# An MLP up projection by seven block products, with the weight sums made by adding DMAs

## The chip, the cores and the metric

The kernel runs on one core of one Trainium2 chip. The metric is the device time of one execution in microseconds, the median of several runs. A profile of one execution has a row for each instruction of the engines: TensorE (PE, its weight loads PEld), VectorE (DVE), ScalarE (ACT), GpSimd (POOL) and SyncE (SP, which issues DMAs).

## What is computed

One layer of a hybrid backbone over 512 latent tokens and 256 context tokens, model width 2048, in float32. The layer projects the modulated tokens, runs bidirectional GLA and mLSTM scans, gates and projects the result back, and adds it to the residual stream. Then follows the MLP, which the change is about:

```python
def conv_ffn(h, rows, cols, w_up, conv_w, conv_b, w_down):
    u = jnp.einsum('btd,df->btf', h, w_up)            # 512 x 2048 by 2048 x 11008
    u_gate, u_val = jnp.split(u, 2, axis=-1)          # 5504 columns each
    g = lax.conv_general_dilated(u_gate.reshape(b, rows, cols, D_FF), ...)   # 3x3 depthwise, 8 x 64 grid
    g = g.reshape(b, t, D_FF) + conv_b
    return jnp.einsum('btf,fd->btd', jax.nn.silu(g) * u_val, w_down)
...
    h2 = rmsnorm(x, g_norm2) * (1 + sc2) + sh2
    x = x + gt2 * conv_ffn(h2, rows, GRID_W, w_up, conv_w, conv_b, w_down)
```

The shifts, scales and gates (sh, sc, gt) come from a vector times a 2048 x 12288 matrix, six regions of 2048 columns. A final RMSNorm ends the kernel.

## The kernel before

All activations lie transposed: 128 channels on the partitions, 512 tokens along a row, so the 2048 channels are 16 tiles (k). A float32 product is made by three faster ones (`mm3`): each operand is split into a high part (`hi`, a cast on ScalarE, line 89) and a low part (`lo`, the rest, a subtraction on VectorE, line 90), and high by high, high by low and low by high are summed in PSUM. `load_split` fetches 512 KB of weights (two k, 512 columns) on SP's queue into one of four buffers `wraw` (tag "raw") and splits it into one of two buffers `whi` and `wlo`. So a split can start only when the chunk two before has been used up, and it has the time of one chunk to be ready.

`unit` runs eight such chunks over four PSUM tiles of 512 tokens: 8 x 4 x 2 x 3 = 192 matmuls. The MLP has 43 column tiles of 128 gate and 128 value columns, taken four at a time: a unit `ug` for the gate, a unit `uv` for the value. Between them VectorE and ScalarE convolve (`cv`: a first tap on ScalarE, eight on VectorE at line 1043, one after another on the same tile), and the product with the value is split into `gh` and `gl`. After two such rounds `down_block` (`dn`) multiplies the eight finished tiles with the down weights, in four blocks of 512 outputs, and `residual` adds them to the stream `x2`, which stays in SBUF. The tail `dl` does the last block in two parts of the tokens so that the norm can begin early.

Beside this run the "fillers": the modulation regions 2 to 5 are sums over weight rows (`raw_m`, `sum_m`), made by VectorE, ScalarE and POOL from 512 KB loads, with a `rate` that says how many fillers a weight chunk brings along. Regions 2, 3 and 4 run beside the heads and the gate and output projections (`ga`, `wo`), region 5 beside the first units of the MLP. Their loads use the same `wraw` buffers as the weights.

A scheduler orders the instructions of each engine at build time, by program order and priority; a waiting instruction then holds up those behind it on its engine.

Of the kernel before, what the change touches and what calls it, by code (L numbers as in the profile page):

```python
# [11 lines left out]
F32 = mybir.dt.float32  # L12
F32R = mybir.dt.float32r
# [5 lines left out]
P = 128  # L19
# [17 lines left out]
QUADS = [4] * 10 + [3]  # L37
GROUPS = [[0, 1], [2, 3], [4, 5], [6, 7], [8, 9, 10]]
# [31 lines left out]
def block_kernel(ctx: ExitStack, tc: tile.TileContext, a: dict, out: bass.AP):  # L70
# [48 lines left out]
    actp = pool(ctx, "actp")  # L119
    yp = pool(ctx, "yp")  # L120
    psA = pool(ctx, "psA", 6, PSUM)
# [16 lines left out]
    def ytile(k, name, shape=(P, T)):  # L138
        return yp.tile(list(shape), F32, name=name, tag=f"y{k}")
# [18 lines left out]
    rate, credit = [0], [0]  # L158

# [82 lines left out]
    def mod_chunk(region, n, kp, parts):  # L242

        name = f"m{region}_{n}_{kp}"
        raw = wraw.tile([P, 2, T], F32, name=f"raw_{name}", tag="raw")
# [12 lines left out]
        if kp == KP - 1:  # L258
            G.tensor_tensor(out=po, in0=po, in1=dv, op=ALU.add)
# [616 lines left out]
    mod_fillers((2, 3, 4), 3)  # L876
# [34 lines left out]
    for h in range(1, 2 * H):  # L911
        if h + 1 < 2 * H:
            accs = [acc(f"a{h + 1}_{g}", BANKS[g]) for g in range(6)]
            steps = project_steps(h + 1, accs)
        else:
            rate[0] = 1.5
# [15 lines left out]
    rate[0] = 1.5  # L932
# [19 lines left out]
    def residual(k, ps, gate, sl=slice(0, T)):  # L952
        xx = x2[k][:, sl]
        V.scalar_tensor_tensor(out=xx, in0=ps, scalar=gate[:, k : k + 1], in1=xx, op0=ALU.mult, op1=ALU.add)
# [27 lines left out]

    sums2 = []
    for n in range(4):
        accs = unit(a["w_out"][n], f"wo{n}", yh, yl)
        with tc.high_priority():
            for i in range(4):
                residual(4 * n + i, accs[i], modc[2])
                square(4 * n + i, sums2, rp, "sq")
# [3 lines left out]
    h2 = ([], [])  # L993
    with tc.high_priority():
        for k in range(KT):
            t = gp.tile([P, T], F32, name=f"h2_{k}", tag="h2")
            sk, bk = modc[4][:, k : k + 1], modc[3][:, k : k + 1]
            h2[0].append(acttile(k, "h", f"h2h{k}"))
            h2[1].append(acttile(k, "l", f"h2l{k}"))
            mul(t, x2[k], r2)  # L1000
            S.activation(h2[0][k], t, AF.Identity, scale=sk, bias=bk)  # L1001
            V.tensor_scalar(out=t, in0=t, scalar1=sk, scalar2=bk, op0=ALU.mult, op1=ALU.add)
            sub(h2[1][k], t, h2[0][k].bitcast(F32))
    st_3.close()
    st_h.close()


    fp = pool(ctx, "fp")
    tp = pool(ctx, "tp", 4)
# [4 lines left out]
    pads = [fp.tile([P, ROWS + 2, GW + 2], F32, name=f"pad{i}") for i in range(4)]  # L1014
    for p in pads:
        G.memset(p, 0.0)
    gs = {}
    LAST = 4 * GROUPS[-1][0]
    glast = fp.tile([P, NF - LAST, P], F32, name="glast")

    def sum_tile(i, name):
        return fp.tile([P, T], F32, name=f"sum{i}_{name}", tag=f"g{'hl'[i]}10")

    rate[0] = 1.5
    fillers += [lambda: None] * 20
    mod_fillers((5,), 2)

    def up_gate(q):
        accs = unit(a["w_up4"][2 * q] if q < 10 else a["w_up3"][0], f"ug{q}", *h2, n=QUADS[q])
        convs = []  # L1030
        for i, ps in enumerate(accs):
            f = 4 * q + i
            with tc.high_priority():
                S.copy(pads[i][:, 1 : ROWS + 1, 1 : GW + 1], ps.rearrange("p (r c) -> p r c", c=GW))
            t = tp.tile([P, T], F32, name=f"cv{f}", tag="cv")
            t3 = t.rearrange("p (r c) -> p r c", c=GW)
            for tap in range(9):
                src = pads[i][:, tap // 3 : tap // 3 + ROWS, tap % 3 : tap % 3 + GW]
                w = cwt[:, f, tap : tap + 1]
                if tap == 0:  # L1040
                    S.activation(t3, src, AF.Identity, scale=w, bias=cbt[:, f : f + 1])  # L1041
                else:
                    V.scalar_tensor_tensor(out=t3, in0=src, scalar=w, in1=t3, op0=ALU.mult, op1=ALU.add)  # L1043
            S.activation(t, t, AF.Silu)
            convs.append(t)
        return convs

    def up_val(q, convs):
        accs = unit(a["w_up4"][2 * q + 1] if q < 10 else a["w_up3"][1], f"uv{q}", *h2, n=QUADS[q])
        for i, ps in enumerate(accs):  # L1050
            f = 4 * q + i
            with tc.high_priority():
                mul(convs[i], convs[i], ps)
                gh = fp.tile([P, T], F32R, name=f"gh{f}", tag=f"gh{f % 8 if q < 10 else 8 + i}")
                gl = fp.tile([P, T], F32R, name=f"gl{f}", tag=f"gl{f % 8 if q < 10 else 8 + i}")
                split(gh, gl, convs[i])
            gs[f] = (gh, gl)
            if f >= LAST:
                S.copy(glast[:, f - LAST, :], convs[i][:, 3 * P :])

    def fspan(qs):
        return [f for q in qs for f in range(4 * q, 4 * q + QUADS[q])]

    def down_block(fs, blk):
        accs = [acc(f"dn{fs[0]}_{blk}_{i}") for i in range(4)]
        for p in range(0, len(fs), 2):
            pair = fs[p : p + 2]
            wh, wl = load_split(a["w_down"][blk][:, pair[0] : pair[0] + len(pair), :], f"d{pair[0]}_{blk}", n=len(pair))
            for i in range(4):
                for ff, f in enumerate(pair):  # L1070
                    mm3(accs[i], wh[:, ff, P * i : P * i + P], wl[:, ff, P * i : P * i + P],
                        gs[f][0], gs[f][1], f == fs[0], f == fs[-1])
        with tc.high_priority():
            for i in range(4):
                residual(4 * blk + i, accs[i], modc[5])

    todo = list(GROUPS)
    for q in range(len(QUADS)):
        convs = up_gate(q)
        if len(todo) > 1 and q > todo[0][-1]:  # L1080
            assert not fillers
            for blk in range(4):
                down_block(fspan(todo[0]), blk)
            todo.pop(0)
        up_val(q, convs)
# [3 lines left out]
    fs = fspan(todo[0])  # L1089
    parts = [slice(0, 3 * P), slice(3 * P, T)]  # L1090
    sums3 = [[], []]
    for blk in range(3):
        down_block(fs, blk)
        for k in range(4 * blk, 4 * blk + 4):
            for pt, sl in enumerate(parts):
                square(k, sums3[pt], fp, f"fq{pt}", sl)
            S.activation(x2[k], x2[k], AF.Copy, scale=gnf[:, k : k + 1])

    wd = []
    for n, f in enumerate(fs):  # L1100
        if n < 10:
            raw = actp.tile([P, T], F32, name=f"raw_dl{f}", tag=f"a{'hl'[n % 2]}{11 + n // 2}")
        else:
            raw = fp.tile([P, T], F32, name=f"raw_dl{f}", tag="wlast")
        wh, wl = acttile(n, "h", f"dlh{f}"), acttile(n, "l", f"dll{f}")
# [5 lines left out]
    for pt, sl in enumerate(parts):  # L1111
# [10 lines left out]
        with tc.high_priority():  # L1122
            for i in range(4):
                residual(12 + i, accs[i], modc[5], sl)
                square(12 + i, sums3[pt], fp, f"fq{pt}", sl)
            r3 = token_rstd(sums3[pt], fp, f"rmsf{pt}", w)
            r3s = fp.tile([P, w], F32, name=f"r3s{pt}", tag=f"r3s{pt}")
# [17 lines left out]
def arrange(x, c, ctx, c_ctx, w_mod, b_mod, g_norm1, g_norm2, w_in, gla_w_lr, gla_b_lr, mlstm_b_gate,  # L1145
# [44 lines left out]
    for d in range(2):  # L1190
# [3 lines left out]
    r["w_up4"] = np.stack([blocks(w_up[:, FF * s + 512 * q : FF * s + 512 * q + 512], 512)  # L1194
                           for q in range(10) for s in range(2)])
    r["w_up3"] = np.stack([blocks(w_up[:, FF * s + 5120 : FF * s + 5504], 384) for s in range(2)])
# [20 lines left out]
```

## Time and profile before

| | |
|---|---|
| median of 3 runs | 2596.1 us (2593.98 to 2598.04) |
| profiled execution | 2598.67 us, its span 2597.0 us |
| PE busy | 2530.0 us, 97%, 12782 matmuls |
| DVE, ACT, POOL busy | 1361.3, 873.7, 225.8 us |
| granted TensorE clock, mean | 0.993 |
| DMA | 321.96 MB, mean 124 GB/s |
| MLP | from 1163.5 us to the end |

Busy times of matmuls overlap: a row's duration is longer than the pace at which such rows follow each other. So the pace is read from the starts of neighbouring rows, or from a stretch with its count. A row of the groups has line, engine, operation, output and inputs, shape and count, then busy time and mean duration in ns, then the idle time before it and what ended it. Names of tiles have their buffer numbers left out.

### The profile page before, as it was taken

What the parts mean: (1) busy time and instruction counts of PE and PEld (TensorE: products, weight loads), DVE (VectorE), ACT (ScalarE), POOL (GpSimd) and SP (SyncE); (2) the same over time, 40 slices, a digit from 0 to 9 for tenths busy, and PEclk for the clock granted to TensorE, in tenths of its full rate; (3) what the DMA queues carried; (4) which work ended last, traced back from release to release, by engine and by line L of the source; (5) the groups of instructions that cost most, each with busy time, mean ns of one, the idle gap of its engine ahead of it and who ended that gap; (6) DMA issues with size and microseconds to landing.
All of it is one profiled execution on the core that took longest, in us unless ns stands there. A gap on an engine that the chain in (4) does not pass through costs nothing.

```text
span 2597.0 us, 31782 instructions
## 1 busy us (share of the span) xinstructions
PE 2530.0 (97%) x12782; PEld 2132.0 (82%) x12782; DVE 1361.3 (52%) x1972; ACT 873.7 (34%) x1289; POOL 225.8 (9%) x179
## 2 busy tenths in 40 slices
PE   6998999999999999999999999999999999999998
PEld 4887898888897887878878888888888888888887
DVE  6566765543344465458576326533653365336643
ACT  4224543333334344334443123312331233123431
POOL 0000000111212323210321000000000000000000
PEclk9999999999999999989999999999999999999999
DMA  8751012231333566633554333333233323333431
GB/s 322 282 204 41 30 44 81 69 96 64 130 119 126 205 233 221 192 121 100 208 186 138 97 98 98 98 97 97 98 97 96 96 95 97 97 97 90 141 90 65
DMA packets 96676, 321.96 MB, mean 124 GB/s; under 512 B 11152, under 2 KB 15504, under 8 KB 96528
## 3 DMA queue, kind: packets, MB, share of 16 engines
q1 hardware_dynamic: 95376, 319.40, 37.5%
q8 instruction: 100, 1.64, 0.3%
q10 hardware_dynamic: 1152, 0.52, 0.1%
q14 instruction: 48, 0.39, 0.0%
HBM read 315.69 MB, written 4.19 MB: 123 GB/s over the span
## 4 chain that ended last, share of the span: by engine, by line
PE 89%; DVE 5%; DMA 3%; issue 1%; ACT 1%; SPq 0%; POOL 0%; DVEq 0%; ACTq 0%; POOLq 0%
PE ug L95 18%; PE uv L95 17%; PE dn L95 17%; PE a L95 16%; PE wo L95 6%; PE ga L95 5%; PE po L95 3%; DMA raw_m<-in_w_mod 2%; PE sl L95 1%; PE dl L95 1%; PE ps_m L95 1%; DVE cv L1043 1%; DMA raw_h<-in_w_heads 1%; PE s L95 0%; PE cst L95 0%
## 5 line engine op out<-in xcount | busy, mean ns | idle before, releaser
L95 PE MATMUL ug<-h2h,hi_ug 128*128 128x512 f32 x688 | 269.0, 392 | 1.6 <-ACT h2h L1001 1.6
L95 PE MATMUL uv<-h2h,lo_uv 128*128 128x512 f32 x688 | 268.8, 391 | 1.6 <-DVE lo_uv L90 1.6
L95 PE MATMUL uv<-h2h,hi_uv 128*128 128x512 f32 x688 | 268.6, 390 | 1.2 <-ACT hi_uv L89 1.2
L95 PE MATMUL ug<-h2l,hi_ug 128*128 128x512 f32 x688 | 268.3, 390 | 0.0
L95 PE MATMUL uv<-h2l,hi_uv 128*128 128x512 f32 x688 | 268.2, 390 | 0.0
L95 PE MATMUL ug<-h2h,lo_ug 128*128 128x512 f32 x688 | 268.2, 390 | 0.0
L95 PE MATMUL dn<-gh,hi_d 128*128 128x512 f32 x644 | 250.5, 389 | 0.0
L95 PE MATMUL dn<-gl,hi_d 128*128 128x512 f32 x644 | 250.5, 389 | 0.0
L95 PE MATMUL dn<-gh,lo_d 128*128 128x512 f32 x644 | 250.5, 389 | 0.0
L1043 DVE SCALAR_TENSOR_TENSOR cv<-pad,cwt,cv 128x512 f32<-128x512 f32 x344 | 242.5, 762 | 10.6 <-ACT cv L1041 9.1
L90 DVE TENSOR_TENSOR lo_ug<-raw_ug,hi_ug 128x1024 fp32r<-128x1024 f32 (+1 forms) x88 | 106.5, 1210 | 240.1 <-ACT hi_ug L89 240.1
L257 POOL TENSOR_TENSOR sum_m<-sum_m,raw_m 128x512 f32<-128x512 f32 x112 | 175.3, 1566 | 578.2 <-ACT raw_m L256 358.4
L90 DVE TENSOR_TENSOR lo_uv<-raw_uv,hi_uv 128x1024 fp32r<-128x1024 f32 (+1 forms) x88 | 105.9, 1203 | 177.5 <-ACT hi_uv L89 177.1
L90 DVE TENSOR_TENSOR lo_d<-raw_d,hi_d 128x1024 fp32r<-128x1024 f32 x82 | 98.8, 1205 | 166.5 <-ACT hi_d L89 165.5
L89 ACT CAST hi_ug<-raw_ug 128x1024 fp32r<-128x1024 f32 (+1 forms) x88 | 90.9, 1033 | 266.6 <-PE ug L95 196.4
L89 ACT CAST hi_d<-raw_d 128x1024 fp32r<-128x1024 f32 x82 | 85.0, 1037 | 280.4 <-PE dn L95 231.8
L255 DVE SCALAR_TENSOR_TENSOR sum_m<-raw_m,csil,sum_m 128x512 f32<-128x512 f32 x112 | 97.6, 871 | 156.1 <-DMA raw_m<-in_w_mod 155.9
L89 ACT CAST hi_uv<-raw_uv 128x1024 fp32r<-128x1024 f32 (+1 forms) x88 | 90.9, 1033 | 246.4 <-PE uv L95 181.3
L95 PEld LDWEIGHTS uv<-h2h,lo_uv 128*128 128x128 f32 x688 | 129.4, 188 | 30.2 <-DVE lo_uv L90 3.2
L95 PEld LDWEIGHTS ug<-h2h,hi_ug 128*128 128x128 f32 x688 | 129.8, 189 | 28.8 <-ACT h2h L1001 1.9
L95 PEld LDWEIGHTS uv<-h2h,hi_uv 128*128 128x128 f32 x688 | 129.5, 188 | 28.3 <-ACT hi_uv L89 1.6
L95 PEld LDWEIGHTS ug<-h2h,lo_ug 128*128 128x128 f32 x688 | 129.6, 188 | 27.2
(308 smaller groups left out, 5178.7 us busy)
## 6 DMA issues: line engine op xcount, KB each, us to landing
raw_m<-in_w_mod SPq DMA_DIRECT2D x192, 512.0 KB, 4.4
raw_ug<-in_w_up SPq DMA_DIRECT2D x80, 512.0 KB, 3.4
raw_uv<-in_w_up SPq DMA_DIRECT2D x80, 512.0 KB, 3.4
raw_d<-in_w_down SPq DMA_DIRECT2D x79, 512.0 KB, 3.5
raw_h<-in_w_heads SPq DMA_DIRECT2D x64, 512.0 KB, 3.4
raw_ga<-in_w_gates SPq DMA_DIRECT2D x32, 512.0 KB, 4.3
raw_wo<-in_w_out SPq DMA_DIRECT2D x32, 512.0 KB, 4.3
xl<-in_xT SPq DMA_DIRECT2D x16, 256.0 KB, 5.1
```

Source lines behind the costliest of these rows:

```text
L89: S.copy(hi, x)
L90: return V.tensor_tensor(out=lo, in0=x, in1=hi.bitcast(F32), op=ALU.subtract).ins
L95: ins = PE.matmul(*args, **kw)
L255: V.scalar_tensor_tensor(out=dv, in0=raw[:, 0, :], scalar=ce, in1=dv, op0=ALU.mult, op1=ALU.add)
L257: G.tensor_tensor(out=po, in0=po, in1=raw[:, 1, :], op=ALU.add)
L1043: V.scalar_tensor_tensor(out=t3, in0=src, scalar=w, in1=t3, op0=ALU.mult, op1=ALU.add)
```

## The change

Each of the last 39 column tiles f is now a 2 x 2 block product: the 2048 input channels in two halves, gate and value as the other two halves of the weights, and the 512 tokens in two halves of 256. Seven products of 1024 channels by 128 columns by 256 tokens (numbered 0 to 6 in the code) and some sums replace eight. Four sums are of weights, four of tokens (made once, `token_sums`, into `bt`), and the rest are of results. The first four column tiles are done plainly (`up_two`), while the token sums are made.

The weight sums are made by DMAs that add to their target, issued by POOL: s1 (its second load added from DRAM), s3 (likewise), then a11 += s1 and a12 += a11 from tiles in SBUF to tiles in SBUF. Product 6 of a tile is put behind product 0 of the next one (`pending`), so TensorE's order is 0 of f, 6 of f - 1, then 1, 3, 2, 5, 4 of f. Before a down block it is not put off. A down group now has seven column tiles (the last one eight).

To make room, the residual stream is written to DRAM (`x2d`) after the output projection; each down block loads four tiles of it into `stage`, adds, and stores them. The last group loads all sixteen back (`x3`). Region 5 of the modulation moves into the gate and output projections, which get four raw buffers of their own for these loads (`mraw3`) and a rate of 2 and 2.25 in place of 1.5.

```diff
-    mod_fillers((2, 3, 4), 3)
+    mod_fillers((2, 3, 4, 5), 3)
...
+    modraw[0] = pool(st_3, "mraw3", 4)
+    rate[0] = 2.25
...
+                residual(x2[k], k, accs[i], modc[2])
+                square(k, sums2, rp, "sq")
+                nc.sync.dma_start(x2d[k], x2[k])
...
+    def up_seven(f, pending):
+        def load(q, i, j, **kw):
+            eng = G if kw else nc.sync
+            eng.dma_start(q, a["w_up"][f - FIRST, i, j].rearrange("p k c -> p (k c)"), **kw)
+        a11, a12, a22 = (wraw.tile([P, KH * P], F32, name=f"q{f}_{n}", tag="raw") for n in range(3))
+        s1, s3 = spare[0][:, f % 2, :], spare[1][:, 0, :]
+        load(s1, 1, 0)
+        load(a11, 0, 0)
+        load(s1, 1, 1, accum_op=ALU.add)
+        load(s3, 1, 0)
+        load(a12, 0, 1)
+        load(s3, 0, 0, accum_op=ALU.add)
+        load(a22, 1, 1)
+        def product(n, src, o, first):
+            wh = whi.tile([P, KH * P], F32R, name=f"hi_q{f}_{n}", tag="hi")
+            wl = wlo.tile([P, KH * P], F32R, name=f"lo_q{f}_{n}", tag="lo")
+            with tc.high_priority():
+                split(wh, wl, src)
+            for k in range(KH):
+                c = slice(P * k, P * k + P)
+                mm3(o, wh[:, c], wl[:, c], *operands[n](k), first and k == 0, k == KH - 1, skip_group_check=True)
...
+        product(0, a11, x, True)
+            S.copy(p1, x)
+        pending()
+        product(1, a12, w, True)
+        G.dma_start(a11, s1, accum_op=ALU.add)
+        G.dma_start(a12, a11, accum_op=ALU.add)
+            add(pad[:, 1 : ROWS // 2 + 1, 1 : GW + 1], rows(w), rows(p1))
+        product(3, s1, v, True)
+            S.copy(p5, v)
+        product(2, a11, x, False)
+            S.copy(u2, x)
+        product(5, a12, v, False)
+            add(pad[:, ROWS // 2 + 1 : ROWS + 1, 1 : GW + 1], rows(v), rows(u2))
+        product(4, s3, x, False)
+            neg_add(val[:, hi], x, p5)
+        def last():
+            product(6, a22, x, False)
+                S.activation(val[:, lo], x, AF.Copy, scale=-1.0)
+            conv(f, pad, val)
+        return last
...
+    def down_block(fs, blk):
+        for i in range(4):
+            nc.sync.dma_start(stage[i], x2d[4 * blk + i])
+        accs = down_products(fs, blk)
+                residual(stage[i], 4 * blk + i, accs[i], modc[5])
+                nc.sync.dma_start(x2d[4 * blk + i], stage[i])
```

VectorE in the middle of the MLP, before, at the end of a value unit (`uv5`) and the start of the next gate unit (`ug6`): `lo_` are the splits, `cv` the convolutions of column tiles 20 to 23, `gl` the low parts of their results.

```order
L1043 SCALAR_TENSOR_TENSOR cv23_13713<-pad3_9430,cwt_9423,cv23_13713 128x512
L90 TENSOR_TENSOR lo_uv5_6_13910<-raw_uv5_6_13908,hi_uv5_6_13909 128x1024
L90 TENSOR_TENSOR lo_uv5_7_13940<-raw_uv5_7_13938,hi_uv5_7_13939 128x1024
L90 TENSOR_TENSOR lo_ug6_0_13994<-raw_ug6_0_13992,hi_ug6_0_13993 128x1024
L83 TENSOR_TENSOR cv20_13677<-cv20_13677,uv5_0_13724 128x512
L83 TENSOR_TENSOR cv21_13689<-cv21_13689,uv5_1_13725 128x512
L90 TENSOR_TENSOR gl20_13970<-cv20_13677,gh20_13969 128x512
```

VectorE now, in one column tile (13): `lo_q13_n` is the split for product n, `cv12` the convolution of the tile before (two, three, two and one taps in a row), `val12` and `pad1` the sums out of PSUM.

```order
L90 TENSOR_TENSOR lo_q13_0_13087<-q13_0_13072,hi_q13_0_13086 128x1024
L1081 SCALAR_TENSOR_TENSOR cv12_13144<-pad0_9546,cwt_9542,cv12_13144 128x512 x2
L1042 SCALAR_TENSOR_TENSOR val12_12850<-x12_12847,part_p5_9648 128x256
L90 TENSOR_TENSOR lo_q12_6_13116<-q12_2_12839,hi_q12_6_13115 128x1024
L1081 SCALAR_TENSOR_TENSOR cv12_13144<-pad0_9546,cwt_9542,cv12_13144 128x512 x3
L90 TENSOR_TENSOR lo_q13_1_13161<-q13_1_13073,hi_q13_1_13160 128x1024
L1081 SCALAR_TENSOR_TENSOR cv12_13144<-pad0_9546,cwt_9542,cv12_13144 128x512 x2
L90 TENSOR_TENSOR lo_q13_3_13192<-spareh_10502,hi_q13_3_13191 128x1024
L1081 SCALAR_TENSOR_TENSOR cv12_13144<-pad0_9546,cwt_9542,cv12_13144 128x512
L86 TENSOR_TENSOR pad1_9547<-w13_13083,part_p1_9647 128x4x64
L90 TENSOR_TENSOR lo_q13_2_13221<-q13_0_13072,hi_q13_2_13220 128x1024
L83 TENSOR_TENSOR cv12_13144<-cv12_13144,val12_12850 128x512
```

The splits stand in the order of the products, and the taps are dealt out between them.

POOL before, from the end of the fillers to the final norm: in between it has nothing.

```order
L257 TENSOR_TENSOR sum1_m5_3_0_10735<-sum1_m5_3_0_10735,raw_m5_3_7_10918 128x512
L259 TENSOR_TENSOR sum1_m5_3_0_10735<-sum1_m5_3_0_10735,sum0_m5_3_0_10734 128x512
L1138 TENSOR_TENSOR x2_2_7960<-x2_2_7960,r3s0_18539 128x384
L1138 TENSOR_TENSOR x2_5_7978<-x2_5_7978,r3s0_18539 128x384
L1138 TENSOR_TENSOR x2_8_7996<-x2_8_7996,r3s0_18539 128x384
```

POOL now, in the column tiles 12 and 13: `spareh` is s1, `sparel` is s3, `q13_0` is a11 and `q13_1` is a12 of tile 13.

```order
L1121 DMA spareh_10502<-in_w_up 128x1024
L1153 DMA q12_0_12837<-spareh_10502 128x1024
L1121 DMA sparel_10503<-in_w_up 128x1024
L1154 DMA q12_1_12838<-q12_0_12837 128x1024
L1121 DMA spareh_10502<-in_w_up 128x1024
L1153 DMA q13_0_13072<-spareh_10502 128x1024
L1121 DMA sparel_10503<-in_w_up 128x1024
L1154 DMA q13_1_13073<-q13_0_13072 128x1024
```

Each tile has four adding DMAs on this queue; the one into s3 stands between the two on tiles in SBUF, and the s1 of the next tile behind them.

More of the change, by code (lines that the diff above doesn't have):

```diff
@@ L981, in token_rstd @@
         return o
+    dr = pool(ctx, "dr", 1, bass.MemoryType.DRAM)
+    x2d = [dr.tile([P, T], F32, name=f"x2d{k}", tag=f"x2d{k}") for k in range(KT)]
     sums2 = []
@@ L992, in block_kernel @@
     assert not fillers
[L993 to L1003, printed above, removed]
     st_3.close()
     st_h.close()
+    st_a.close()
+    KH, TH = KT // 2, T // 2
     fp = pool(ctx, "fp")
-    tp = pool(ctx, "tp", 4)
+    tp = pool(ctx, "tp", 2)
     cwt = fp.tile([P, NF, 9], F32, name="cwt")
@@ L1013, in block_kernel @@
     nc.sync.dma_start(cbt, a["conv_b"])
-    pads = [fp.tile([P, ROWS + 2, GW + 2], F32, name=f"pad{i}") for i in range(4)]
+    pads = [fp.tile([P, ROWS + 2, GW + 2], F32, name=f"pad{i}") for i in range(2)]
     for p in pads:
         G.memset(p, 0.0)
-    gs = {}
[L1018 to L1032, printed above, removed]
-            with tc.high_priority():
[L1034 to L1051, printed above, removed]
-            with tc.high_priority():
[L1053 to L1059, printed above, removed]
@@ new lines, in block_kernel @@
+    with tc.high_priority():
+        for k in range(KT):
+            t = x2[k]
+            sk, bk = modc[4][:, k : k + 1], modc[3][:, k : k + 1]
+            mul(t, t, r2)
+            for sl, (h, l) in halves(k):
+                S.activation(h, t[:, sl], AF.Identity, scale=sk, bias=bk)
+            V.tensor_scalar(out=t, in0=t, scalar1=sk, scalar2=bk, op0=ALU.mult, op1=ALU.add)
+            for sl, (h, l) in halves(k):
+                sub(l, t[:, sl], h.bitcast(F32))
+    assert not fillers
@@ L1100, in block_kernel @@
     for n, f in enumerate(fs):
[L1101 to L1105, printed above, removed]
+        raw = gp.tile([P, T], F32, name=f"raw_dl{f}")
+        wh, wl = (gp.tile([P, T], F32R, name=f"dl{i}{f}") for i in "hl")
         nc.sync.dma_start(raw, a["w_down"][3][:, f, :])
```

159 lines of the change are left out of this document (127 added, 32 removed).

## The prediction

> **What bounds the kernel now.** I read the page first for the engine that carries the span, then the chain that ended last in order of time, then the stretch in which the MLP runs.
>
> ```profile
> span 2597.0 us, 31782 instructions
> PE 2530.0 (97%) x12782; PEld 2132.0 (82%) x12782; DVE 1361.3 (52%) x1972; ACT 873.7 (34%) x1289; POOL 225.8 (9%) x179
> PE 89%; DVE 5%; DMA 3%; issue 1%; ACT 1%; SPq 0%; POOL 0%; DVEq 0%; ACTq 0%; POOLq 0%
> ```
>
> TensorE is 89% of the chain. In the MLP it is nearly all of it; these rows of the chain have start, length, engine and tile:
>
> ```profile
> 1163.54 46.03 PE ug L95 x192
> ...
> 1289.00 5.18 DMA raw_m<-in_w_mod
> ...
> 1393.25 87.04 PE dn L95 x384
> 1480.29 43.52 PE uv L95 x192
> 1523.81 43.52 PE ug L95 x192
> ```
>
> From 1393 on, units of four accumulators follow each other without a gap. 192 matmuls of 512 columns take 43.52 us, so the pace is 43.52/192 = 0.2267 us. (A row's own duration, 0.39 us, is longer because matmuls overlap.) Before 1393 the five units from 1163.54 to 1393.25 take 229.7 us where 5 x 43.52 = 217.6 would do: here the modulation sums ("raw_m") still run.
>
> **The change: matmuls.** A column tile of gate and value had 2 x 16 x 3 = 96 matmuls of 512 columns. It now has 7 x 8 x 3 = 168 of 256. What such a matmul costs in a stream is shown by the head projections:
>
> ```profile
> 658.71 0.28 PE L95 MATMUL a<-hi_h,hTh 128*128 128x256 f32 x1
> ...
> 661.46 0.28 PE L95 MATMUL a<-hi_h,hTl 128*128 128x256 f32 x1
> ```
>
> These are the first and last of 24 in a row: (661.46 - 658.71)/23 = 0.1196 us, somewhat over half of 0.2267. A product of 24 takes 2.87 us, and seven take 20.1. All 43 tiles before: 43 x 96 x 0.2267 = 935.8 us. After: 39 x 20.1 = 783.6, and for the four tiles done plainly 2 x 4 x (48 x 0.1196 + 24 x 0.2267) = 89.4, together 873.0. **Term 1: -62.8 us.** One eighth fewer columns would give 117 us on all 43 tiles; the shorter matmul's fixed part and the four plain tiles take nearly half of it. The down projection has the same products in smaller groups, so I put it at zero.
>
> **The modulation sums of the last gate** leave the MLP. Of the 12.1 us of excess before 1393, 2.5 belong to the first unit (46.03 against 43.52) and stay, and four reductions of 0.79 us only move. **Term 2: -6.4.** They go into the gate and output projections, with four raw buffers of their own:
>
> ```profile
> 928.00:990.00 62.00, 59.92 (x266) 48.71 (x265) 41.82 (x44) 30.77 (x44) 19.61 (x13) 1.00 0.78 264
> 1052.00:1137.00 85.00, 85.00 (x384) 70.33 (x384) 44.24 (x52) 31.16 (x39) 26.58 (x16) 1.00 0.61 198
> ```
>
> Columns: stretch, length, busy time of PE, PEld, DVE, ACT, POOL, clock, DMA share, GB/s. Even at 264 GB/s TensorE lost 2 of 62 us. A half more of the sums will cost something: **term 3: +3** (0 to 12; a gain is excluded, since at most 3 us are idle there).
>
> **The splits.** Each product needs its weights split: a high part on ScalarE, then a low part on VectorE, into the buffer that the product two earlier leaves. A product's cover was 24 x 0.2267 = 5.44 us and becomes 2.87.
>
> ```profile
> 1501.66 0.39 PE L95 MATMUL uv<-h2h,lo_uv 128*128 128x512 f32 x1
> ...
> 1501.86 1.05 ACT L89 CAST hi_uv<-raw_uv 128x1024 fp32r<-128x1024 f32 x1 [4.38 <-PE uv L95]
> ...
> 1502.95 1.23 DVE L90 TENSOR_TENSOR lo_uv<-raw_uv,hi_uv 128x1024 fp32r<-128x1024 f32 x1 [4.22 <-ACT hi_uv L89]
> ```
>
> The chunk begins at 1501.66; the split for the next one starts 0.20 later and ends at 1504.18, 2.52 us in. The first matmul with low weights is the third, whose weights are loaded one matmul ahead, so the slack becomes 2.87 + 0.12 - 2.52 - 0.04 = 0.43 us. Any VectorE work that holds a split up longer stops TensorE. What stands between is the convolution:
>
> ```profile
> L1043 DVE SCALAR_TENSOR_TENSOR cv<-pad,cwt,cv 128x512 f32<-128x512 f32 x344 | 242.5, 762 | 10.6 <-ACT cv L1041 9.1
> L868 DVE SCALAR_TENSOR_TENSOR ob<-po,dn,ob 128x256 f32<-128x256 f32 x16 | 7.7, 484 | 2.0 <-DVE dn L864 0.5
> 1297.90 3.08 DVE cv L1043 x4
> 1302.13 1.21 DVE L90 TENSOR_TENSOR lo_uv<-raw_uv,hi_uv 128x1024 fp32r<-128x1024 f32 x1
> 1303.27 4.05 DVE L1043 SCALAR_TENSOR_TENSOR cv<-pad,cwt,cv 128x512 f32<-128x512 f32 x6
> ```
>
> Taps on one tile follow at 3.08/4 = 0.77 us, and a low part holds VectorE 1.14 us (1302.13 to 1303.27). Free between two low parts: 2.87 - 1.14 = 1.73. Between those of products 0 and 6 stand two taps and a 256-column sum (1.54 + 0.48), between those of 6 and 1 three taps (2.31): 0.29 + 0.58 over, less 0.43 of slack, is 0.44 us a tile. The other gaps hold less. **Term 4: 39 x 0.44 = +17** (0 if taps overlap as the six in 4.05 us do, 34 if the slack isn't there).
>
> **The adding DMAs.** The trace has no DMA that adds and none issued by POOL. The nearest rows are plain transfers of the same 512 KB:
>
> ```profile
> raw_m<-in_w_mod SPq DMA_DIRECT2D x192, 512.0 KB, 4.4
> raw_ug<-in_w_up SPq DMA_DIRECT2D x80, 512.0 KB, 3.4
> 59.53 9.04 DMA raw_h<-in_w_heads
> 60.00:100.00 40.00, 39.26 (x322) 32.15 (x322) 24.65 (x49) 8.98 (x16) 0.00 (x0) 1.00 0.81 300
> 1500.00:1543.00 43.00, 43.00 (x192) 35.59 (x191) 14.83 (x16) 10.72 (x12) 0.00 (x0) 1.00 0.31 97
> ```
>
> They land in 3.4 us on a quiet path, 4.4 on a busy one, 9.04 at the most crowded. At 300 GB/s and a share of 0.81, 512 KB keep the 16 engines 0.81 x 1.75 = 1.42 us. An add reads its target as well, so I take 3.4 + 1.42 + 1.0 (busy path) = 5.8 us, called D, near the middle row; the ends are 3.4 and 9.04.
>
> Count from the start of product 0 of a tile. Its low part is ready at 2.52 - 2.87 = -0.35; then a11 += s1 may go, and a12 += a11 after it and after the low part of product 1 (2.87 + 2.52 + 0.7 of VectorE's delay = 6.1). The high part of product 5, made from a12, must start by 11.5 + 0.2 + 0.43 = 12.1. So two adds in a row fit if -0.35 + 2D is at most 12.1, D at most 6.2; one after 6.1 fits at nearly the same D. Beyond, TensorE waits 2D - 12.45 a tile. At D = 5.8: nothing. Where no product 6 stands between 0 and 1 (tile 4 and the first after each down group, six times) all is due 2.87 earlier and the wait is 2D - 9.6 = 2.0. **Term 5: +12** (0 to 33 x 5.6 + 6 x 8.5 = 236). The adds from DRAM (s1, s3) have more time: s1 is doubled, and s3 is loaded from the end of one product 4 to the next, some 15 us. On POOL's queue an add that waits holds up the ones behind it, and there the next in line is the one that product 5 waits for.
>
> [...]
>
> **Smaller things.** At the six ends of a group product 6 follows product 4 on the same PSUM tile and waits for the 256-column sum out of it: 0.16 for the last matmul to end + 0.48 + two releases of 0.04 (the low part at 1502.95 starts so long after the high part's end), **term 6: 6 x 0.75 = +4.5**. VectorE must make the token sums during the plain tiles, 64 operations of 256 columns:
>
> ```profile
> L557 DVE COPY vn<-a 128x256 f32<-128x256 f32 x14 | 5.9, 421 | 7.4 <-ACT kn L556 7.4
> 1163.00:1253.00 90.00, 89.46 (x385) 73.87 (x386) 73.07 (x102) 40.62 (x51) 11.87 (x9) 0.97 0.36 117
> x<-in_xT SPq DMA_DIRECT2D x16, 256.0 KB, 4.5
> L954 DVE SCALAR_TENSOR_TENSOR x<-dn,mod,x 128x512 f32<-128x512 f32 x75 | 55.2, 748 | 29.6 <-PE dn L95 29.6
> ```
>
> 64 x 0.42 = 27 us on an engine that was busy 73 of 90: **term 7: +3** (0 to 15), since two tiles' convolutions can slip. The residual stream in DRAM I put at zero: a block's store, the next block's load into the same place and four sums take 4.5 + 4.5 + 4 x 0.75 = 12 us, under a block of 7 x 12 x 0.2267 = 19 us, and the weights behind them on SP's queue are for the block after that. Without that cover it is up to 12 us at each of five groups.
>
> **Sum**: -62.8 - 6.4 + 3 + 17 + 12 + 4.5 + 3 = -29.7. The profiled execution took 2598.7 us for its span of 2597.0; 2598.7 - 29.7 = 2569.0. It lay 2.6 over the median of the runs, so 2566.4.
>
> **Rivals.** *No stalls*: taps overlap, D is under 4.8, and terms 3 to 7 vanish: 2598.7 - 69.2 - 2.6 = 2527. For it: the uninterrupted units after 1393; against it: 0.43 us of slack. *The adds are late*: two adds on tiles in SBUF stand in series, and product 5 waits. It turns the change slower from 33 x (2D - 12.45) + 12 x (D - 5.8) = 30, D = 6.55; at D = 7.5 it costs 84 + 20, so 2670. For it: 9.04 us at a crowded moment, and an issue by POOL that no row prices; against it: that was a burst at 300 GB/s. *The DMA engines become the bound*: 5 plain loads and 4 adds of two reads are 13 readings of 512 KB a tile. At 1.42 us that is 18.5 of 20.5 us; at 0.31 x 5.4 = 1.68, the price at 97 GB/s, it is 21.8, and 39 x 1.3 = 51 us more give 2617. Against it: the share falls per byte as load rises. *POOL's issues wait for VectorE*: an issue held for one low part makes D 5.8 + 1.23 = 7.03, which costs 53 + 15, so 2634. For it: VectorE will be busy about 0.8 of the time in this stage; against it: POOL issues nothing in the rows before. [...]
>
> **Chances.** The forecast 0.42 (2527 to 2592), no stalls 0.13, late adds 0.25, DMA bound 0.12, POOL held 0.08. About 0.2% (5 us) is what a measurement of this kernel can tell from no change. The first two are faster, as is a sliver of the third (0.02): 0.57; 0.02 same; 0.41 slower. The range goes from 2525 to 2670: above it lies about half of the late adds, below it next to nothing. The likeliest case's own range is 2527 to 2592.
>
> **What would show it.** In the profile after: 256-column matmuls of a product 0.12 us apart; TensorE waits for "lo" of product 1 of some 0.4 us a tile; adds landing in 5 to 6 us; no wait of ScalarE's "hi" for a DMA except after a down group. I am wrong if a tile takes over 21.3 us ((2596 - 2566)/39 above 20.5), and the row of waits will say for which: ScalarE on an add (late adds), a DMA share near 1 (DMA bound), POOL idle with its inputs ready (held). If the tile takes 20.1, terms 4 and 5 were fear.

## The result, and the profile after

The changed kernel takes 2641.5 us (median of 4 runs, 2629.4 to 2644.3), the kernel before 2597.1 on the same chip. The ratio is 1.0163, with a 95% interval of 1.0129 to 1.0198: slower by 44 us, where 30 us faster was forecast. The profiled execution has a span of 2642.1 us.

These rows of the page have each engine's busy time, and for two DMA queues the packets, the megabytes and the share of the 16 DMA engines' time. They answer to the rows of TensorE before (2530.0 us, 97%); on the queue called software_dynamic stands what GpSimd issues, on q1 what SP issues.

```profile
span 2642.1 us, 39392 instructions
PE 2502.5 (95%) x15758; PEld 2240.7 (85%) x15758; DVE 1592.3 (60%) x2297; ACT 1018.1 (39%) x1559; POOL 369.8 (14%) x341
q1 hardware_dynamic: 129072, 390.20, 42.9%
q0 software_dynamic: 22464, 81.80, 17.4%
```

TensorE is busy for 27.5 us less, and the span is 45 us longer: time went into waits. The 156 adding transfers on q0 keep the 16 engines 0.174 x 2642.1/156 = 2.95 us each, plain ones on q1 0.429 x 2642.1/744 = 1.52 us per 512 KB (390.2 MB are 744 such). The view of waits, for TensorE and then for the others (waiter, tile and line, then what ended the wait: total us, times, longest), says at which place:

```profile
PE v L95 <- ACT part_p L1159: 42.4, 22, 5.0
PE v L95 <- DVE lo_q L90: 11.6, 28, 0.5
PE dn L95 <- ACT hi_d L89: 6.4, 6, 1.1
```

```profile
ACT hi_q L89 <- DMA q<-q: 130.7, 37, 7.8
POOL q L1154 <- DVE lo_q L90: 103.7, 31, 5.5
```

`v` is the PSUM tile of products 3 and 5. In 22 column tiles product 5 stands still for up to 5.0 us, in others for under half a microsecond. Its own split is late, because in 37 of 39 tiles ScalarE waits for a transfer from tile to tile (`q<-q`), which is a12 += a11. (The first row names the copy into `part_p`, since ScalarE makes that copy right behind the late high part.) The chain that ended last shows one such tile (start, length, what):

```profile
2181.20 2.83 PE x L95 x24
...
2194.31 1.23 DVE lo_q L90
2195.54 0.39 issue
2195.93 9.16 DMA q<-q
...
2205.19 1.05 ACT hi_q L89
...
2207.55 4.28 PE v L95 x21
```

An undisturbed product takes 2.83 us. Product 5 waits for a12's add of 9.16 us and for its split (TensorE stands still for 2.46 us ahead of its first matmul and 0.48 ahead of its third), and then itself takes 4.28 for 21 of its matmuls. Busy time by stretch around that place (columns as in the prediction; the clock is the last but two) shows why:

```profile
2196.00:2203.00 7.00, 7.00 (x62) 7.00 (x61) 4.91 (x7) 2.00 (x4) 0.80 (x1) 1.00 0.91 206
2208.00:2211.40 3.40, 3.40 (x18) 3.40 (x17) 1.23 (x2) 0.24 (x1) 0.00 (x0) 0.50 0.91 169
2211.40:2216.00 4.60, 4.60 (x41) 4.60 (x40) 3.46 (x6) 2.82 (x3) 0.86 (x1) 1.00 0.54 209
```

After the wait the granted clock is 0.50 for 3.4 us, ahead of it and behind it 1.00: this stall is paid a second time, as slow matmuls. The rows of DMA issues (KB, median us from issue to landing) and GpSimd's timeline give the adds:

```profile
sparel<-in_w_up POOLq DMA_DIRECT2D x39, 512.0 KB, 7.9
q<-spareh POOLq DMA_DIRECT2D x39, 512.0 KB, 5.1
q<-q POOLq DMA_DIRECT2D x39, 512.0 KB, 6.9
```

```profile
2189.65 0.87 POOL L1153 DMA_DIRECT2D q<-spareh  x1 [5.15 <-DVE lo_q L90]
2192.34 0.87 POOL L1121 DMA_DIRECT2D sparel<-in_w_up  x1 [1.82 <-DMA sparel<-in_w_up]
2195.93 0.87 POOL L1154 DMA_DIRECT2D q<-q  x1 [2.73 <-DVE lo_q L90]
...
2214.56 0.86 POOL L1153 DMA_DIRECT2D q<-spareh  x1 [7.89 <-DVE lo_q L90]
```

a11 += s1, the adding load of s3 and a12 += a11 are issued within 6.3 us, and the last of them lands at 2205.09: three adds in 15.4 us, 5.1 each. The next tile begins its adds 24.9 us after this one, where 20.1 was hoped for.

### The profile page after: what moved, and what is told of

It reads as the page before. It is cut to its first block, busy times and chain, and to the rows that moved or that the text cites. A ratio compares the mean times of both kernels' runs of the same rounds, so it can differ in the third digit from the quotient of the medians.

```text
span 2642.1 us, 39392 instructions
## 1 busy us (share of the span) xinstructions
PE 2502.5 (95%) x15758; PEld 2240.7 (85%) x15758; DVE 1592.3 (60%) x2297; ACT 1018.1 (39%) x1559; POOL 369.8 (14%) x341
## 5 line engine op out<-in xcount | busy, mean ns | idle before, releaser
L89 ACT CAST hi_q<-q 128x1024 fp32r<-128x1024 f32 x195 | 204.9, 1051 | 438.9 <-DMA q<-q 130.7
L90 DVE TENSOR_TENSOR lo_q<-q,hi_q 128x1024 fp32r<-128x1024 f32 x195 | 238.4, 1223 | 169.1 <-ACT hi_q L89 165.8
L95 PE MATMUL a<-hi_h,hTh 128*128 128x256 f32 x512 | 151.9, 297 | 0.0
L95 PEld LDWEIGHTS dn<-gh,hi_d 128*128 128x128 f32 x656 | 123.2, 188 | 32.8 <-ACT hi_d L89 7.6
L95 PE MATMUL a<-hi_h,hTl 128*128 128x256 f32 x512 | 146.7, 287 | 0.0
L95 PE MATMUL a<-lo_h,hTh 128*128 128x256 f32 x512 | 146.5, 286 | 0.0
L95 PEld LDWEIGHTS dn<-gh,lo_d 128*128 128x128 f32 x656 | 123.2, 188 | 25.5
L95 PEld LDWEIGHTS dn<-gl,hi_d 128*128 128x128 f32 x656 | 123.2, 188 | 25.4
L95 PE MATMUL v<-b1h,hi_q 128*128 128x256 f32 x312 | 101.0, 324 | 42.4 <-ACT part_p L1159 42.4
L95 PE MATMUL v<-b1h,lo_q 128*128 128x256 f32 x312 | 102.5, 328 | 12.0 <-DVE lo_q L90 11.6
```

The costliest lines, as they stand in the source:

```text
L89: S.copy(hi, x)
L90: return V.tensor_tensor(out=lo, in0=x, in1=hi.bitcast(F32), op=ALU.subtract).ins
L95: ins = PE.matmul(*args, **kw)
```

## Experiments

**1. Both sums between tiles left out.** Lines 1153 and 1154 go:

```
-        G.dma_start(a11, s1, accum_op=ALU.add)
-        G.dma_start(a12, a11, accum_op=ALU.add)
```

> The two adds on tiles in SBUF (a11 += s1, a12 += a11) are left out, so products 2 and 5 use a11 and a12 as loaded. Theory A (the two adds stand in series and product 5 waits for the second): a tile falls from some 21.8 us to 20.1 to 20.6, a tile after a down group from 24.5 to about 17.5, together 90 to 100 us less: 2540 to 2555. Theory B (the DMA engines are the bound; 4 of 13 readings of a tile are gone): also less, since a tile needs 9 readings of 1.4 to 1.7 us, at most 15. Theory C (the 256-column products or the VectorE work are slower than thought): little change, 2620 or more.

Measured 2548.2 us, ratio to the kernel before 0.9818 [0.9794, 0.9843]. Without these two transfers the changed kernel is 93 us faster, and 47 us faster than the kernel before.

**2. Only a12 += a11 left out.**

```
-        G.dma_start(a12, a11, accum_op=ALU.add)
```

> Leaves out one addition, a12 += a11, so that product 5 runs on the block a12 alone and the result is not the reference's; a11 += s1 stays as an adding DMA between tiles in SBUF, and so do the second loads from DRAM. Theory (the second of two adds in series lands too late, the first one lands in time): nearly all of the stall before product 5 goes, about 1.7 us in each of 33 steady tiles and 5 us at each of six restarts, so 2641 - 85 = 2555 us, within 2545 to 2575, close to the kernel without both adds (2548). Rival (any add between SBUF tiles is late, so that the wait moves to product 2): 2590 to 2625, with waits of product 2's split for a11.

Measured 2547.7, 0.9820 [0.9801, 0.9840]. Leaving out this one transfer is worth the whole 93 us; with a11 += s1 as the only add between tiles nothing is lost against experiment 1. GpSimd's timeline shows what a tile takes when no add is late:

```profile
2172.69 0.87 POOL L1153 DMA_DIRECT2D q<-spareh  x1 [5.66 <-DVE lo_q L90]
...
2192.61 0.88 POOL L1153 DMA_DIRECT2D q<-spareh  x1 [5.48 <-DVE lo_q L90]
```

19.9 us, against 20.1 in the prediction's first term.

**3. Both sums between tiles by GpSimd's own addition.**

```
-        G.dma_start(a11, s1, accum_op=ALU.add)
-        G.dma_start(a12, a11, accum_op=ALU.add)
+        G.tensor_tensor(out=a11, in0=a11, in1=s1, op=ALU.add)
+        G.tensor_tensor(out=a12, in0=a12, in1=a11, op=ALU.add)
```

> The two sums on tiles in SBUF are made by POOL's tensor_tensor in place of DMAs; the result is the same. From POOL's 128x512 adds (1.57 to 1.6 us) one of 1024 columns should take 3.1 to 3.2 us. Theory A: lo of product 0, 3.2, lo of product 1, 3.2 is over before product 5's split, so the wait goes: 2545 to 2575. Theory B: the DMA engines are relieved by 4 of 13 readings, so the same. Rival D: POOL's adds slow VectorE's two-input operations beside them, and the splits come late: VectorE's lo grows from 1.22 us and the time stays at 2600 or more.

Measured 2681.3, 1.0336 [1.0315, 1.0358]: slower still. GpSimd's timeline, then VectorE's at the same moment:

```profile
2230.58 2.83 POOL L1153 TENSOR_TENSOR q<-q,spareh 128x1024 f32<-128x1024 f32 x1 [6.29 <-DVE lo_q L90]
```

```profile
2230.41 3.56 DVE L1081 SCALAR_TENSOR_TENSOR cv<-pad,cwt,cv 128x512 f32<-128x512 f32 x2
...
2235.36 2.32 DVE L1081 SCALAR_TENSOR_TENSOR cv<-pad,cwt,cv 128x512 f32<-128x512 f32 x3
```

Two taps that start beside GpSimd's addition take 3.56 us, three others 2.32, which is 1.55 for two. VectorE loses some 2 us beside this addition of 2.83, and the splits come late behind it (TensorE waits 106 us for VectorE ahead of the products, 1.9 at most at a time).

**4. The second loads of s1 and s3 left out,** so that the two sums between tiles are the only adding transfers (products 3 and 4 run on single blocks).

```
-        load(s1, 1, 1, accum_op=ALU.add)
-        load(s3, 0, 0, accum_op=ALU.add)
```

> The second loads of s1 and s3, which add from DRAM, are left out; the two adds on tiles in SBUF stay. Theory A in its bare form (an add takes 6.9 us whatever runs beside it): the wait of product 5 stays, 2630 or more. Theory A with contention (the second add lands late because the other transfers share its engines and its queue): the add lands in 5 to 5.5 us in place of 6.9, most of the wait goes, 2560 to 2590. Theory B (the engines' total is the bound): the same gain as leaving out the two adds in SBUF, 2540 to 2560, with waits for plain loads gone too.

Measured 2581.6, 0.9951 [0.9934, 0.9967]. Both sums now land in 4.7 us (rows of DMA issues), and only five waits of product 5 are left, one behind each down group, 20.3 us in all:

```profile
q<-spareh POOLq DMA_DIRECT2D x39, 512.0 KB, 4.7
q<-q POOLq DMA_DIRECT2D x39, 512.0 KB, 4.7
```

Behind the first down group the chain has:

```profile
1427.96 6.84 DMA q<-spareh
1435.43 6.93 DMA q<-q
```

So two things make the stall: in steady tiles the two adding loads, which cost a12's add 2.2 us of its 6.9; behind a down group the two sums in series, each some 2 us longer there than in the median, though no other add is in this kernel. SP's stores and loads of the residual stream run beside them; no run leaves these out, so that they are the reason is not shown.

**5. s3's adding load issued behind a12's add** instead of ahead of it.

```
-        load(s3, 0, 0, accum_op=ALU.add)
...
-        G.dma_start(a12, a11, accum_op=ALU.add)
+        ins = G.dma_start(a12, a11, accum_op=ALU.add).ins
+        with tc.issue_after(ins):
+            load(s3, 0, 0, accum_op=ALU.add)
```

> Only the order on POOL's queue is changed: the add into s3 is issued behind a12 += a11 in place of ahead of it. Theory A with the queue as the cause (a12's add is processed behind s3's on the same rings): it lands 1 to 2 us earlier, 2590 to 2615. Theory A with the plain loads as the cause, or theory B: no change beyond 0.5%, 2630 to 2655.

Measured 2640.2, 1.0169 [1.0141, 1.0197]: no change. But the delay changed hands (rows of DMA issues):

```profile
q<-q POOLq DMA_DIRECT2D x39, 512.0 KB, 4.6
sparel<-in_w_up POOLq DMA_DIRECT2D x39, 512.0 KB, 9.0
```

a12's add is down from 6.9 to 4.6, and s3's load, now behind it, is up from 7.9 to 9.0. Product 4, which needs s3, waits in its stead: the waits of its PSUM tile `x` for a split or a copy grow from some 2 to 27 us. Whichever of the two is issued second pays.

**6. The kernel before with region 5's modulation sums in the gate and output projections,** as in the change, and the MLP as it was.

```
-    mod_fillers((2, 3, 4), 3)
+    mod_fillers((2, 3, 4, 5), 3)
...
-            rate[0] = 1.5
+            rate[0] = 2
...
-    rate[0] = 1.5
+    modraw[0] = pool(st_3, "mraw3", 4)
+    rate[0] = 2.25
```

> The kernel before with one part of the change alone: the modulation sums of region 5 move from the MLP into the gate and out projections, with the change's rates and its own raw buffers; the MLP stays as it was. Theory (these sums are what made the stretch ahead of the MLP 18 us longer in the kernel after): +13 to +18 ahead of the MLP, -6.4 in the MLP, so 2602 us, within 2597 to 2608. Rival (the prediction's +3): 2591, within 2588 to 2594. Second rival (the stores of the residual stream to DRAM made it longer): no more than +4 ahead of the MLP, 2590 to 2594 here too, and the out projection as long as in the kernel before.

Measured 2602.8, 1.0022 [1.0012, 1.0032]. From the first matmul of the gate projection to the last of the output projection it takes 398.2 us (768.8 to 1167.0), the kernel before 383.1 (769.1 to 1152.2): 15 us more, of which some 9 come back behind it, in the MLP. One stretch of the kernel before, then the same of this one:

```profile
930.00:1010.00 80.00, 76.94 (x340) 62.48 (x339) 49.70 (x51) 36.21 (x50) 24.30 (x15) 1.00 0.70 242
```

```profile
930.00:1010.00 80.00, 75.12 (x324) 60.20 (x323) 60.64 (x65) 41.12 (x60) 31.25 (x20) 0.96 0.78 277
```

In the same 80 us 16 matmuls fewer are done, which at 0.2267 is 3.6 us. TensorE's busy time falls by 1.8 us only; the rest is the clock, 0.96 where it was 1.00. The stores of the residual stream are not in this kernel, so they are not the cause.

**7. Product 1 ahead of the held-back product 6.**

```
-        pending()
         product(1, a12, w, True)
+        pending()
```

> Product 1 runs ahead of the held-back product 6 of the tile before, so that in a steady tile both adds are issued one product (2.87 us) earlier against product 5; at the six restarts nothing is held back and nothing changes. Theory (latency of the two adds in series is the bound): steady stalls of 0 to 5 us before product 5 shrink by up to 2.87 us, 33 tiles by about 1.5 us, so 2590 us, within 2575 to 2610, and product 5 still waits about 5 us at each restart. Rival (the transfers' own rate is the bound, so that they only end later): 2632 to 2650. Second rival: product 1's split now waits for the buffer of the half-split that product 5 of the tile before uses, or the evictions of x come late: the wait moves to products 1 or 6, 2620 to 2650.

Measured 2656.1, 1.0237 [1.0219, 1.0254]. My theory fell: what starts earlier did not land earlier. In the rows of DMA issues a12's add takes 7.7 us instead of 6.9. Why the sum is worse than no gain I did not settle.

**8. a12 += a11 by VectorE.** The last adding DMA goes, and behind product 2 in the program stands:

```
+        with tc.high_priority():
+            add(a12, a12, a11)
```

> a12 += a11 is made by VectorE (one tensor_tensor of 128x1024, estimated 1.15 to 1.25 us from the same size of the low half's subtraction, 1.22) ahead of the split of product 5; a11 += s1 stays a DMA. Theory (series of two transfers is what stalled): the stall before product 5 goes, and VectorE has 2.5 us of room in a 20.1 us tile: 2560 us, within 2548 to 2580. Rival (VectorE has no room: splits come late behind taps and the add): 1.2 us in each of 39 tiles, 2595 to 2610, with waits of PE for lo_q behind the add.

Measured 2578.9, 0.9938 [0.9923, 0.9953]. Steady tiles run at 20.0 us. The chain behind a down group shows what is left:

```profile
2102.04 6.50 DMA q<-spareh
...
2111.05 5.06 PE v L95 x22
```

There VectorE, and the split behind it, wait for a11's add of 6.50 us, and the product after the wait takes 5.06 instead of 2.83.

**9. Both sums between tiles by VectorE.** Neither is a DMA; `add(a11, a11, s1)` stands ahead of product 2, `add(a12, a12, a11)` behind it.

> Both additions between SBUF tiles are made by VectorE; the two adding loads from DRAM stay. Theory: no stall for a transfer is left in the loop, VectorE gets 2.4 us more in a tile, of which a part holds up splits: 2562 us, within 2548 to 2585, no better than one add on VectorE. Rival (VectorE becomes late): 2600 to 2640, with waits of PE for lo_q growing from about 20 to over 60 us.

Measured 2543.2, **0.9801 [0.9786, 0.9815]**: faster than the kernel before, and by 98 us than the changed one. Its page, and the steady part of its MLP:

```profile
span 2545.2 us, 39245 instructions
PE 2463.1 (97%) x15758; PEld 2214.0 (87%) x15758; DVE 1668.8 (66%) x2375; ACT 1023.9 (40%) x1559; POOL 301.7 (12%) x263
```

```profile
1430.00:2500.00 1070.00, 1064.69 (x7513) 999.55 (x7512) 784.10 (x945) 449.13 (x599) 64.21 (x75) 1.00 0.65 188
```

TensorE is busy for all but 5 of 1070 us, at full clock; VectorE's two sums find room (73% busy). Against the changed kernel TensorE is busy for 39.4 us less (2502.5 - 2463.1), and the span is 96.9 shorter. The mean granted clock is 0.988 of 2545.2 us here, 0.977 of 2642.1 there, so the low clock makes at most 0.023 x 2642.1 - 0.012 x 2545.2 = 30 us of the 96.9; the rest is waits, but for some 9 us of busy time that I did not assign.

**10. Single transfers on the quiet chip.** In experiment 9's kernel, during the last down projection, seven transfers of 512 KB on GpSimd's queue, each waiting for the one before.

```
+            G.dma_start(z1, z0)
+            G.dma_start(z1, z0, accum_op=ALU.add)
+            G.dma_start(z1, z0, accum_op=ALU.add)
+            G.dma_start(z1, z_blk, accum_op=ALU.add)
+            G.dma_start(z1, z_blk, accum_op=ALU.add)
+            G.dma_start(z1, z_blk)
+            G.dma_start(z1, z0)
```

(`z_blk` lies in DRAM.)

> The kernel with both tile sums on VectorE, and beside it, in the last down projection where the other transfers have ended, seven transfers of 512 KB on GpSimd's queue, each waiting for the one before: a copy from tile to tile, two adds from tile to tile, two adding loads from DRAM, a plain load from DRAM, a copy from tile to tile. Theory (the adds were slow for lack of room beside other transfers): an add alone takes 3.0 to 4.0 us from issue to landing, against 5.1 and 6.9 in the loop. Rival (an adding transfer is slow by itself): 4.5 to 5.5 us alone, and well over the copy's time.

GpSimd's timeline (the copy and the add before these rows met the last weight loads):

```profile
2472.55 0.87 POOL L1242 DMA_DIRECT2D z<-z  x1 [4.16 <-DMA z<-z]
2477.48 0.86 POOL L1243 DMA_DIRECT2D z<-in_w_up  x1 [4.07 <-DMA z<-z]
...
2488.66 0.55 POOL L1245 DMA_DIRECT2D z<-in_w_up  x1 [4.71 <-DMA z<-in_w_up]
2492.70 0.54 POOL L1246 DMA_DIRECT2D z<-z  x1 [3.48 <-DMA z<-in_w_up]
```

From issue to next issue an add between tiles takes 4.9 us, an adding load 5.6 ((2488.66 - 2477.48)/2), a plain load 4.0. The landing times of the seven go from 2.9 to 5.2, with a median of 4.5. An add is slower by itself than a plain transfer, which the theory had wrong; but alone it is far from 6.9. Busy time in the stretch of the add, then of the plain load:

```profile
2472.55:2477.48 4.93, 4.93 (x23) 4.11 (x22) 4.51 (x10) 4.45 (x10) 0.87 (x1) 1.00 0.56 106
2488.66:2492.70 4.04, 4.04 (x19) 3.35 (x18) 0.47 (x1) 0.00 (x0) 0.56 (x2) 1.00 0.42 130
```

The share of the DMA engines times the length is the time for which a transfer keeps all 16: 0.56 x 4.93 = 2.8 us for the add, 0.42 x 4.04 = 1.7 for the plain load.

**11. Only a11 += s1 by VectorE,** a12 += a11 left as a DMA (the mirror of experiment 8).

```
-        G.dma_start(a11, s1, accum_op=ALU.add)
+        with tc.high_priority():
+            add(a11, a11, s1)
```

> The mirror of the kernel with one sum on VectorE: here a11 += s1 is made by VectorE and a12 += a11 stays a DMA from tile to tile, so that one adding transfer is left ahead of product 5 and it starts as soon as product 1's block is split. Theory (two transfers in series are what comes late; one, even at 7 to 9 us, ends in time): tiles of 19.9 to 20.1 us and no long stall at the restarts, 2550 us, within 2540 to 2570. Rival (a12's add at 7 to 9 us is late by itself, beside the other transfers): stalls before product 5 stay in steady tiles, 2590 to 2625.

Measured 2584.9, 0.9951 [0.9934, 0.9968], between the two forecasts. The series is gone, but steady tiles still take some 20 to 25 us.

**12. Experiment 11 with product 1 ahead of product 6.** The edits of 7 and 11 together.

> As the kernel with only the first tile sum on VectorE (2585), and product 1 runs ahead of the held-back product 6 of the tile before, so that a12's add, which there was issued once product 1's block was split, starts one product (2.87 us) earlier against product 5. Theory (in a steady tile the loop product 5, splits of the next products up to product 1, a12's add of 7 us, split for product 5 is what sets 20.0 to 24.7 us): the loop gets 2.87 us shorter, tiles of 19.9 us, 2555 us, within 2545 to 2570. Rival (an add that starts earlier lands no earlier, because the engines are shared, which is why the same move gained nothing with both adds as DMAs): 2578 to 2595.

Measured 2594.1, 1.0005 [0.9992, 1.0018]: the theory fell again, and the rival gave the reason. GpSimd's timeline of experiment 11, then of 12, at the same tile:

```profile
2153.96 0.88 POOL L1121 DMA_DIRECT2D sparel<-in_w_up  x1 [7.72 <-DMA sparel<-in_w_up]
2156.23 0.87 POOL L1155 DMA_DIRECT2D q<-q  x1 [1.40 <-DVE lo_q L90]
```

```profile
2150.61 0.88 POOL L1121 DMA_DIRECT2D sparel<-in_w_up  x1 [7.92 <-DMA sparel<-in_w_up]
2151.35 1.03 POOL L1155 DMA_DIRECT2D q<-q  x1
```

In 11 a12's add is issued 2.27 us behind s3's and lands after 7.31, in 12 it is issued 0.74 behind and lands after 9.01 (both from the chain). From s3's issue to a12's landing it is 9.6 and 9.75 us. Moved forward, the add just stands longer behind s3's.

**13. Pairs of transfers on the quiet chip,** as in experiment 10, with two independent adds one right behind the other and then a copy behind each, and at the end an add and an adding load one right behind the other.

```
+            G.dma_start(z1, z0, accum_op=ALU.add)
+            G.dma_start(z3, z2, accum_op=ALU.add)
+            G.dma_start(z3, z2)
+            G.dma_start(z1, z0)
...
+            G.dma_start(z3, z0, accum_op=ALU.add)
+            G.dma_start(z1, z_blk, accum_op=ALU.add)
```

> The kernel with both tile sums on VectorE, and in the last down projection, where the other transfers have ended, transfers of 512 KB on GpSimd's queue in pairs: two independent tile-to-tile adds issued one right behind the other, a copy behind each, an add of half the size, a plain load from DRAM with an add behind it, and at the end a tile-to-tile add with an adding load from DRAM right behind it. Theory (adding transfers of one queue are done one after the other, each some 4.5 us, so that four in a tile fill 20 us): the second add of a pair lands about 9 us after its issue, the first after 4.5. Rival (they run side by side and are slow only beside many other transfers): both land within 5 to 6.5 us.

```profile
2471.55 0.88 POOL L1244 DMA_DIRECT2D zz<-zz  x1
2472.14 1.19 POOL L1243 DMA_DIRECT2D zz<-zz  x1
2477.10 0.55 POOL L1245 DMA_DIRECT2D zz<-zz  x1 [3.77 <-DMA zz<-zz]
2481.48 0.54 POOL L1246 DMA_DIRECT2D zz<-zz  x1 [3.83 <-DMA zz<-zz]
```

The first copy, released by the first add, goes 5.55 us after that add's issue; the second, released by the second add, 9.34 after its own, 4.4 behind the first. But a weight load on SP's queue (issued at 2473.64) still runs beside this pair. Beside the last one, issued at 2494.76 and 2495.32, nothing else moves (rows of DMA issues in that stretch, then busy time):

```profile
zz<-zz POOLq DMA_DIRECT2D x1, 512.0 KB, 4.8
zz<-in_w_up POOLq DMA_DIRECT2D x1, 512.0 KB, 7.2
2496.00:2502.00 6.00, 6.00 (x28) 4.95 (x27) 1.32 (x3) 1.09 (x3) 0.53 (x1) 1.00 0.98 175
```

The second add lands 3.0 us behind the first, not 4.4: the two stand in line, and the step is about the time for which an add keeps the engines (2.8 to 2.95 us). The 16 engines are taken up (0.98) by these two transfers alone; my estimate from this share is that a second queue would find no room on them, but no run put adds on another queue.

## Why the prediction was wrong

The direction was wrong; the time lay inside the range, in the rival of the late adds, which had a chance of 0.25.

**Term 5 failed: +12 forecast, 93 measured** (changed kernel less experiment 1). Its place was right, product 5 on a12, and so was the moment at which a12's add can be issued: 6.45 us behind a11's in the prediction's count (-0.35 to 6.1), 6.28 in the tile shown. What failed is the time of the add itself. It was given a D of its own, 5.8 us, so that it would land at 11.9 and be in time at 12.1, and the loads from DRAM were set aside because they "have more time". But it stands in line with the transfers issued ahead of it (experiments 4, 5, 12, 13), s3's add above all: it takes 6.9 us in the median and 9.16 in the tile shown, which by the prediction's own count is 6.1 + 9.16 - 12.1 = 3.2 us too late. TensorE waits 2.46 + 0.48 there. For a lone add 5.8 was even too much (4.5 in experiment 10). The prediction named the order on POOL's queue and priced only its waits before an issue, not the time behind it.

From one product 1 to the next (the rows of tile `w` in both traces), the five tiles behind down groups lose 37 us against experiment 1, 7.5 each where the term had 2.0, and the 33 others 58 us together, where it had nothing.

**The restarts**, the tiles behind down groups, failed by D as well. Behind a down group a tile takes 24.8 us (2144.52 to 2169.36 on GpSimd's timeline) where 17.3 do in experiment 2. The two adds there take 14.8 together where 2D = 11.6 was put, and that is not s3's doing: in experiment 4, without s3's add, they take 14.4 (1427.96 to 1442.36 in the chain). By the prediction's rule 14.8 gives a wait of 14.8 - 9.6 = 5.2 us; TensorE's rows have 4.41 and 0.19 there, and the granted clock is 0.50 again (2160.2 to 2167.0).

**The clock was not in the sum at all.** The waits of 2.46 and 0.48 us shown, 2.9 in two pieces, are followed by 3.4 us at 0.50, so that 21 matmuls of product 5 take 4.28 us where 21 x 0.118 = 2.5 would do; at most 30 of the 97 us between the changed kernel and experiment 9 are this. In the tile behind a down group above, on waits of 4.41 and 0.19, it is 6.8 us at 0.50. Experiment 3 has 106 us in waits of at most 1.9 us before the products, and a granted clock of 0.992 where the changed kernel has 0.977 and the kernel before 0.993: those waits, though many, did not bring the clock down.

**Term 3 was too small: +3 forecast, about +15** (experiment 6; in the changed kernel the two projections take 397.7 us, 773.0 to 1170.7). The bound was read from TensorE's idle time in one stretch, and about half of the cost in the stretch shown came as a lower clock.

**Term 2** was near: in experiment 6 some 9 us come back in the MLP, 6.4 forecast. **Term 4 was not there.** 17 us were put down for taps between splits; without late adds a tile takes 19.9 us, the slack and the taps' overlap hold, and 0 was the right end. **Term 1 held**: 2.83 us a product, 2.87 forecast. **Term 6** is near: six waits of 1.07 us at the group ends instead of 0.75, though for the split of a down weight, not for PSUM. **Term 7 held**: the plain tiles take 91.8 us (1181.3 to 1273.1) against 89.4 + 3. The residual stream's loads and stores hold up no product directly in the rows; what they cost the adds beside them at the restarts no run shows.

Without term 5 the forecast was -41.7 and experiment 1 measured -46.8. The differences add up: +81 in term 5, +12 in term 3, -17 in term 4 make 76, against a miss of 75 (2641.5 - 2566.4).

Of the rivals, GpSimd's issues being held by VectorE is not what happened: an issue takes 0.86 to 0.89 us in nearly all rows, and with the adds made elsewhere (experiment 9) issues beside a busier VectorE hurt nothing. The engines as the bound came nearer than its chance of 0.12: with 2.95 us for an add and 1.52 for a plain load a tile's four adds and five loads need 4 x 2.95 + 5 x 1.52 = 19.4 us (18.5 forecast) of the 20.1, so that nothing of the line can be made up. But the sum alone does not decide. Experiments 8 and 11 leave out one add each, so both need 16.5 us by these figures; 8, which leaves out the last of the chain, has steady tiles of 20.0 us, 11, which leaves out the first, still has tiles up to 25.

## What to carry to other kernels

Cost a chain of DMAs by what stands in line with it, not by one transfer's latency: list every transfer that is issued between the first and the last of the chain, the plain ones of the other queue too (in experiment 13 the copies behind two adds went 4.4 us apart beside a weight load of SP's, while the pair alone landed 3.0 apart), and add up the time for which each keeps the 16 engines (here some 3 us for an adding transfer of 512 KB, 1.5 for a plain one). A sum that a waiting engine needs within a few microseconds belongs on an engine with room (VectorE, 1.2 us) and not on a transfer of 5 to 9. And price a stall of TensorE with the slow matmuls behind it too: here 1.8 us on a wait of 2.9, while waits of at most 1.9 (experiment 3) left the clock at 0.992.

## What was not expected of the hardware

- An adding transfer of 512 KB keeps the 16 DMA engines some 2.8 us, a plain load 1.7. Two adds issued 0.6 us apart with nothing beside them land 3.0 us apart (4.8 and 7.2 from issue), and the engines' share is 0.98 meanwhile. Alone an add between tiles takes 4.5 from issue to landing, a plain copy as little as 2.9.
- The granted clock falls to 0.50 for 3.4 us after waits of 2.46 and 0.48 us; on waits of 4.41 and 0.19 it is at 0.50 for 6.8 us.
- GpSimd's addition of 128x1024 takes 2.83 us and makes two taps on VectorE take 3.56, where the three beside them take 2.32, so that it cost more than the transfers that it replaced (2681 against 2641 us).
